# Expert outputs kept by slot and gathered at the end, in place of a scatter that adds into the residual

## Chip, cores and metric

One core of one Trainium2 chip runs the whole program. The metric is the device time of one execution in microseconds (us); a lower number is better. The engines are TensorE (PE, with its weight loads as PEld), VectorE (DVE), ScalarE (ACT), GpSimd (POOL) and SyncE (SP). Every engine executes its own instructions in order. DMAs are issued by SP (queue q1 of the profile) or by POOL (queue q0); both kinds run on the same 16 DMA engines.

## The reference, cut to what matters

One decoder layer over 1,024 tokens and 16 meta tokens, with 1,024 features: a token mixer (attention beside a gated delta rule), a layer norm, a mixture of experts, and a last layer norm. The change concerns the mixture of experts and what follows it. Each token takes one of four groups and in it two of eight experts, so each of the 1,024 tokens has two (expert, weight) pairs out of 32 experts.

```
combine = group_onehot[:, :, None] * (g_val * within)[:, None, :]
y = jnp.zeros((t, x.shape[1]), jnp.float32)
for gi in range(N_GROUPS):
    h = jax.nn.silu(x @ w1[sl]) * (x @ w3[sl])
    y = y + jnp.einsum("tef,efd->td", h * combine[:, gi, :, None], w2[sl])
...
h = layer_norm(DEEPNORM_ALPHA * h + ffn, ln2_g[i], ln2_b[i])
```

## The kernel before

Everything is float32; for TensorE each operand is split into a rounded high part and a low rest, and three products are summed. The last third of the program is `phase4`, and it is written in a fixed order (a manual schedule), not chosen by a scheduler.

Routing gives each (token, choice) pair a slot: `pose` is its place in its expert's list, `oh` its expert as a one-hot row, `ix[:, e]` the token that stands in each of the 128 slots of expert `e` (a number past the end for an empty slot), `gsl` the weight of that slot. On average 64 of 128 slots are filled (2,048 pairs over 32 experts). An expert with more than 128 tokens would go through a separate branch (`overflow`), which is compiled in and not taken with these inputs.

The expert loop runs over `e` from 0 to 31. The token rows of expert `e` are fetched by an indirect DMA from `h1d`, the layer's normalised rows in DRAM (`gather`, L1498, three buffers `xg`). PE transposes them, multiplies by w1 and w3 (`up`), ACT and DVE make the SwiGLU, and `down` multiplies by w2. The weights, 3 MiB for each expert, come in three 1 MiB loads by SP (`load_raw`, L1449) into a ring of 17 tiles, so up to 5.67 experts ahead; ACT and DVE split them into high and low parts. In the pass for `e` the product of expert `e - 1` is weighted and copied into one of two buffers `y` (`evac`, ACT L1566 and DVE L1567), and POOL sends it off (`scatter`, L1571): an indirect DMA that adds 128 rows of `y` into the rows of `res` in DRAM. `res` was filled earlier with the same rows as `h1d`.

The outputs of the last two experts (30 and 31) are not scattered. They stay on chip, and PE adds them in the last stage by a product with one-hot matrices (`pf`, L1738).

The last stage, `finish`, takes eight tiles of 128 tokens. SP loads `yt0` to `yt7` from `res` after the last scatter (L1637). For a tile, `total` adds `pf` and sums the row (DVE L1747), `square` (ACT L1751, L1752), `rstd` (DVE L99, POOL L100), `shift` (DVE L1758), `scale` (ACT), `gain` (DVE L1764), and `store` (an add on DVE or POOL, L1767, and SP's store L1768). The list `TO` sets the stagger of these steps over the tiles, and `TV` names the tiles whose last add is on DVE.

Between the loop and `finish` stands the branch for overflow (`If(nv > 0)`, L1662). Where it isn't taken, POOL still waits for its own DMAs and then raises the semaphores by what the branch would have raised (INC_SWDGE_SEM).

Of the kernel before, what the change touches and what calls it, by code (L numbers as in the profile page):

```python
# [17 lines left out]
P = 128  # L18
D = 1024
# [17 lines left out]
TV, TO = (4, 6, 7), (0, 0.75, 1.25, 2.5, 3.25, 4, 4.75)  # L37
# [9 lines left out]
YB = 2  # L47
SPK = ()
# [31 lines left out]
class Trunk:  # L80
# [738 lines left out]
    def phase2(self):  # L819
# [242 lines left out]
        self.res = self.dram.tile([SEQ, D], F32, name="res")  # L1062
# [107 lines left out]
        def s1(t):  # L1170
            c = T[t]
            ht = c["ht"]
            for s in range(2):
                omm(t, s, 0, 1.0)
                yield
            if t < 6:
                rs = self.ln_stats(ht, P)
                self.ln_apply(ht, P, rs, ht)
                for v, w in ((O["g1"], ALU.mult), (O["b1"], ALU.add)):
                    nc.vector.tensor_tensor(ht, ht, v, op=w)  # L1180
            else:
                c["st"] = mv, rs = self.ln_stats(ht, P, raw=True)
                yield
                nc.vector.scalar_tensor_tensor(rs[:, 1:2], mv[:, 0:1], -1.0, rs[:, 0:1], op0=ALU.mult, op1=ALU.mult)
                self.ln_apply(ht, P, rs, ht)
                for v, w in ((O["g1"], ALU.mult), (O["b1"], ALU.add)):
                    for h in range(2):
                        (nc.gpsimd if h in LH[t - 6] else nc.vector).tensor_tensor(
                            ht[:, h * F:(h + 1) * F], ht[:, h * F:(h + 1) * F], v[:, h * F:(h + 1) * F], op=w)
            nc.sync.dma_start(self.h1d[t * P:(t + 1) * P, :], ht)  # L1190
            nc.sync.dma_start(self.res[t * P:(t + 1) * P, :], ht)
# [282 lines left out]
    def phase4(self):  # L1474
# [155 lines left out]
        g2, b2 = [fp.tile([P, D], F32, name=n) for n in ("g2", "b2")]  # L1630
        for v, n in ((g2, "ln2_g"), (b2, "ln2_b")):
            (nc.gpsimd if GQ else nc.sync).dma_start(v, self.bcast(a[n], D))
        yts = [fp.tile([P, D], F32, name=f"yt{t}") for t in range(NT)]

        def load_res(eng):
            for t in range(NT):
                eng.dma_start(yts[t], self.res[t * P:(t + 1) * P, :])  # L1637

        load_res(nc.sync)
        ys.append([fp.tile([P, D], F32R, name=f"y{x}") for x in "hl"])  # L1640
# [17 lines left out]
    def overflow(self, item, ps, xo, reload):  # L1658
# [3 lines left out]
        with tc.If(nv > 0), self.pool("ovf", "left") as vp:  # L1662
# [20 lines left out]
            nc.vector.scalar_tensor_tensor(sl, q, -128.0, pose, op0=ALU.mult, op1=ALU.add)  # L1683
            pa = ps.tile([P, 512], F32, name="py", bufs=3)
# [28 lines left out]
            nc.gpsimd.memset(xo, 0.0)  # L1713
            xi = vp.tile([P, 1], I32, name="xi")
            xg = vp.tile([P, 1], F32, name="xg")
            with tc.For_i(0, nv) as i:
# [3 lines left out]
                nc.vector.tensor_copy(xg, g16[:, bass.ds(i, 1)])  # L1720
                item(a["w13"][bass.ds(ev, 1)].rearrange("o p k f -> p (o k) f"),
                     a["w2"][bass.ds(ev, 1)].rearrange("o p k f -> p (o k) f"),
                     xi, xg, xo)
            reload(nc.gpsimd)

    def finish(self, fp, g2, b2, yts, oh, ys, sq):
# [3 lines left out]
        with self.psum("psf") as ps, tc.manual_schedule():  # L1730
# [26 lines left out]
            def shift(t):  # L1757
                nc.vector.tensor_tensor(rs[t][:, 1:2], st[t][:, 1:2], rs[t][:, 0:1], op=ALU.mult)  # L1758
# [73 lines left out]
```

## Time and profile before

| what | us |
|---|---|
| median of 3 runs | 1203.93 (1203.56 to 1207.17) |
| the profiled execution, its own time | 1209.06 |
| its span, first to last instruction | 1207.3 |
| PE busy | 1086.3 |
| DVE busy | 865.7 |
| ACT busy | 625.4 |
| POOL busy | 308.6 |

The profiled execution's own time is 1.8 us over its span and 5.1 us over the median. Busy times are sums over the program; what a change in the expert loop or in the last stage is worth is read from those stretches, about 830 to 1160 and 1160 to 1207 of the span.

### The profile page before, as it was taken

To read this page: it belongs to the slowest core of one execution; us is meant where nothing else is said; L and a number is where in the kernel's file an instruction comes from. 1 tells how busy PE (TensorE), PEld (TensorE's weight loads), DVE (VectorE), ACT (ScalarE), POOL (GpSimd) and SP (SyncE) were. 2 spreads that over 40 slices of the span, in tenths; PEclk is the share of its full clock that TensorE was granted. 3 is DMA by queue.
4 is the path that set the end of the run, shared out by engine and by line. 5 is a ranking of instruction groups with operands and counts; after the bars stand their busy time and mean duration, and the time that the engine had idled before them with its cause. 6 is when DMAs were issued, how large, how long until landed. Compare 5 with 4: busy or idle time off the path is not lost. (4 is left out here: it accounts for less than half of the span.)

```text
span 1207.3 us, 19744 instructions
## 1 busy us (share of the span) xinstructions
PE 1086.3 (90%) x7029; PEld 925.2 (77%) x7029; DVE 865.7 (72%) x1661; ACT 625.4 (52%) x1310; POOL 308.6 (26%) x380
## 2 busy tenths in 40 slices
PE   6999999999899979899899999839999889888981
PEld 4999999999899958778677777837776666666761
DVE  7941357989433248999757687778988787787978
ACT  3443346845223245655456463236776566566854
POOL 3523103402000023444333230011222122122315
PEclk9999999999989979999979999769999999999996
DMA  7411124465896577876657653957999999997453
GB/s 284 175 62 45 50 93 125 150 189 188 241 253 187 171 259 213 250 233 190 196 133 187 239 181 114 401 220 256 359 335 328 316 321 320 321 323 265 83 195 139
DMA packets 111287, 259.22 MB, mean 215 GB/s; under 512 B 32804, under 2 KB 62252, under 8 KB 98386
## 3 DMA queue, kind: packets, MB, share of 16 engines
q1 hardware_dynamic: 101680, 239.57, 59.0%
q0 software_dynamic: 9216, 17.28, 6.2%
q8 instruction: 57, 0.93, 0.3%
q10 hardware_dynamic: 290, 1.07, 0.2%
q14 instruction: 44, 0.36, 0.1%
HBM read 205.44 MB, written 68.72 MB: 227 GB/s over the span
## 5 line engine op out<-in xcount | busy, mean ns | idle before, releaser
L184 PE MATMUL pj<-hTh,wfh 128*128 128x346 f32 (+1 forms) x480 | 156.5, 326 | 0.0
L186 PE MATMUL pj<-hTh,wfl 128*128 128x346 f32 (+1 forms) x480 | 156.0, 325 | 0.0
L185 PE MATMUL pj<-hTl,wfh 128*128 128x346 f32 (+1 forms) x480 | 156.0, 325 | 0.0
L1571 POOL DMA_INDIRECT res<-y,ix x30 | 51.0, 1699 | 234.7 <-DVE y L1567 168.0
L879 DVE TENSOR_TENSOR_SCAN mm<-mm,zero 128x272 f32<-128x272 f32 (+3 forms) x64 | 89.6, 1413 | 20.8 <-ACT mm L866 18.4
L184 PEld LDWEIGHTS pj<-hTh,wfh 128*128 128x128 f32 x480 | 91.1, 190 | 0.4 <-issue 0.3
L185 PEld LDWEIGHTS pj<-hTl,wfh 128*128 128x128 f32 x480 | 91.1, 190 | 0.2
L186 PEld LDWEIGHTS pj<-hTh,wfl 128*128 128x128 f32 x480 | 91.1, 190 | 0.1
L1462 DVE TENSOR_TENSOR w13l<-raw,w13h 128x512 fp32r<-128x512 f32 x144 | 88.9, 684 | 0.0
L1530 PE MATMUL ph<-w13h,xh 128*128 128x512 f32 x192 | 88.5, 461 | 0.0
L177 PE MATMUL pj<-wvh,hTl 128*128 128x256 f32 (+3 forms) x280 | 79.1, 285 | 3.6 <-DVE hTl L95 3.6
L176 PE MATMUL pj<-wvl,hTh 128*128 128x256 f32 (+3 forms) x280 | 79.1, 285 | 2.2 <-DVE wvl L95 2.2
L175 PE MATMUL pj<-wvh,hTh 128*128 128x256 f32 (+3 forms) x280 | 79.7, 288 | 0.2 <-ACT hTh L94 0.2
L1461 ACT ACTIVATE w13h<-raw 128x512 fp32r<-128x512 f32 x144 | 77.8, 625 | 0.0
L1532 PE MATMUL ph<-w13h,xl 128*128 128x512 f32 x192 | 75.1, 391 | 0.0
L1531 PE MATMUL ph<-w13l,xh 128*128 128x512 f32 x192 | 74.9, 390 | 0.0
L864 PE MATMUL z<-qk 128*128 128x416 f32 (+6 forms) x224 | 60.7, 378 | 7.0 <-ACT kuw L776 4.4
L866 ACT ACTIVATE mm<-z 128x512 f32<-128x512 f32 (+1 forms) x80 | 44.2, 565 | 42.0 <-PE z L864 36.8
L870 POOL TENSOR_SCALAR_AFFINE_SELECT mm<-mm 128x128 f32<-128x128 f32 x64 | 36.5, 576 | 114.6 <-ACT mm L866 114.2
L94 ACT ACTIVATE xh<-tp 128x512 fp32r<-128x512 f32 x64 | 31.4, 490 | 58.8 <-DVE xf L1517 53.0
L1462 DVE TENSOR_TENSOR w2l<-raw,w2h 128x512 fp32r<-128x512 f32 x96 | 60.0, 687 | 2.3 <-ACT w2h L1461 0.2
L900 ACT ACTIVATE wt<-tp 128x512 f32<-128x512 f32 (+1 forms) x80 | 41.6, 556 | 27.9 <-PE tp L899 27.3
(425 smaller groups left out, 2932.6 us busy)
## 6 DMA issues: line engine op xcount, KB each, us to landing
raw<-in_w SPq DMA_DIRECT2D x72, 1024.0 KB
qk<-qkd SPq DMA_DIRECT2D x16, 520.0 KB
ht<-hscr SPq DMA_DIRECT2D x16, 512.0 KB
qk<-qkd SPq DMA_DIRECT2D x16, 392.0 KB
kqvd<-y SPq DMA_DIRECT2D x12, 520.0 KB
wfr<-in_w_gdn SPq DMA_DIRECT2D x12, 512.0 KB
wo4h<-in_w SPq DMA_DIRECT2D x6, 1024.0 KB
wo4l<-in_w SPq DMA_DIRECT2D x6, 1024.0 KB
```

The source lines that it names most:

```text
L175: nc.tensor.matmul(o[:p, :n], xh, wh[:, kt, ws], start=(kt == 0), stop=False)
L176: nc.tensor.matmul(o[:p, :n], xh, wl[:, kt, ws], start=False, stop=False)
L177: nc.tensor.matmul(o[:p, :n], xl, wh[:, kt, ws], start=False, stop=(kt == KT - 1))
L184: nc.tensor.matmul(o[:, :n], wh[:, kt], self.hTh[:, kt, c0:c0 + n], start=(kt == 0), stop=False)
L185: nc.tensor.matmul(o[:, :n], wh[:, kt], self.hTl[:, kt, c0:c0 + n], start=False, stop=False)
L186: nc.tensor.matmul(o[:, :n], wl[:, kt], self.hTh[:, kt, c0:c0 + n], start=False, stop=(kt == KT - 1))
L879: nc.vector.tensor_tensor_scan(mm[:, c0:c1][:, ::-1], mm[:, c0:c1][:, ::-1], self.zero1.to_broadcast([P, c1 - c0]), 1.0, op0=ALU.mult, op1 ...
L1461: nc.scalar.activation(wh, raw, AF.Copy)
L1462: (nc.gpsimd if k in pool else nc.vector).tensor_tensor(wl, raw, wh.bitcast(F32), op=ALU.subtract)
L1530: nc.tensor.matmul(ph, xh[:, kt], wh, start=False, stop=False)
L1531: nc.tensor.matmul(ph, xh[:, kt], wl, start=False, stop=False)
L1532: nc.tensor.matmul(ph, xl[:, kt], wh, start=False, stop=(kt == ks[-1]))
```

## The change

Expert outputs no longer go into the residual's rows. `ysd` is a new DRAM tensor of 30 x 128 rows; `keep` stores the whole `y` of expert `e` as rows `e * 128` to `e * 128 + 127`, with a plain DMA from POOL. `res` and its eight stores are gone. `fi` holds, for each token and choice, its row in `ysd` (128 x expert + slot, or past the end where the expert is 30 or 31); DVE computes it in five instructions before the loop. In the last stage SP loads `yt` from `h1d`, and `combine` adds two rows for each token of a tile with two indirect DMAs whose destination is `yt` in on-chip memory. Five tiles (`GE`) are combined ahead of the overflow branch, the other three from inside `shift`. All eight last adds go to DVE. The gather for a later expert moves behind the transposes of its pass, and the loads of the gain and bias rows move from POOL to SP.

```
-TV, TO = (4, 6, 7), (0, 0.75, 1.25, 2.5, 3.25, 4, 4.75)
+TV, TO = (0, 1, 2, 3, 4, 5, 6, 7), (0, 0.75, 1.25, 2.5, 3.25, 4, 4.75)
+GE = 5
...
-        self.res = self.dram.tile([SEQ, D], F32, name="res")
+        self.ysd = self.dram.tile([(NE - 2) * P, D], F32, name="ysd")
+        self.ovd = self.dram.tile([16 * P, D], F32, name="ovd")
...
-            nc.sync.dma_start(self.res[t * P:(t + 1) * P, :], ht)
...
-        def scatter(y, yi):
-            nc.gpsimd.indirect_dma_start(out=self.res, out_offset=bass.IndirectOffsetOnAxis(ap=yi, axis=0),
-                                         in_=y, in_offset=None, bounds_check=SEQ - 1, oob_is_err=False,
-                                         compute_op=ALU.add)
+        def keep(y, e):
+            nc.gpsimd.dma_start(self.ysd[e * P:(e + 1) * P, :], y)
+
+        def combine(src, fi, n, t):
+            for k in range(2):
+                nc.gpsimd.indirect_dma_start(out=yts[t], out_offset=None, in_=src,
+                                             in_offset=bass.IndirectOffsetOnAxis(ap=fi[:, t, k:k + 1], axis=0),
+                                             bounds_check=n * P - 1, oob_is_err=False, compute_op=ALU.add)
...
+        nc.vector.tensor_tensor(ev, self.oh, self.slots[:, None, None, :NE].to_broadcast([P, NT, 2, NE]), op=ALU.mult)
+        nc.vector.tensor_reduce(fv, ev, axis=AX, op=ALU.add)
+        nc.vector.scalar_tensor_tensor(fv, fv, float(P), self.pose, op0=ALU.mult, op1=ALU.add)
+        nc.vector.tensor_scalar(fo, self.pose, float(P), 4096.0, op0=ALU.is_ge, op1=ALU.mult)
+        nc.vector.tensor_tensor(fi, fv, fo, op=ALU.add)
         xt = xsplit(xpose(XB[0]))
+        gat_(XN)
...
         for e in range(NE):
-            gat_(e + XN)
...
+                gat_(e + 1 + XN)
...
-                    yo, yi = down(act, pcs.pop(e - 1)), self.ix[:, e - 1:e]
-                    scatter(evac(yo, self.gsl[:, e - 1:e]), yi)
+                    keep(evac(down(act, pcs.pop(e - 1)), self.gsl[:, e - 1:e]), e - 1)
...
+        for t in range(NT):
+            nc.sync.dma_start(yts[t], self.h1d[t * P:(t + 1) * P, :])
...
+        for t in range(GE):
+            combine(self.ysd, fi, NE - 2, t)
         evac2(down(act, pcs.pop(NE - 1)), self.gsl[:, NE - 1:], ys[1])
...
-        self.finish(fp, g2, b2, yts, oh, ys, sq)
+        self.finish(fp, g2, b2, yts, oh, ys, sq, lambda t: t < NT and combine(self.ysd, fi, NE - 2, t))
...
             def shift(t):
+                more(t + GE)
                 nc.vector.tensor_tensor(rs[t][:, 1:2], st[t][:, 1:2], rs[t][:, 0:1], op=ALU.mult)
```

POOL at the end of the expert loop, before: the scatters of experts 27 to 29 (each waits for DVE, ACT and one DMASW, the semaphore of the scatter ahead of it) and the two row loads.

```order
L1571 DMA res<-y,ix 1024x1024 [waits DMASW1_49,DVE_49,Activation_49]
L1571 DMA res<-y,ix 1024x1024 [waits DMASW3_49,DVE_49,Activation_49]
L1571 DMA res<-y,ix 1024x1024 [waits DMASW4_49,DVE_49,Activation_49]
L1632 DMA g_12653<-in_ln_g 128x1024 [waits DMAHW2_49,DMAHW1_49,DMAHW6_49,DMAHW0_49,DMAHW7_49,DMASW6_49,DVE_49]
L1632 DMA b_12654<-in_ln_b 128x1024
```

The same place after the change: the stores of experts 27 to 29, then the gathers for tiles 0 to 4, of which tiles 0, 1 and 4 are shown (`yt_12597`, `yt_12598`, `yt_12601`). DMASW names with other numbers than the neighbour's are older DMAs that used the same semaphore.

```order
L1572 DMA ysd<-y 128x1024 [waits DVE_49,Activation_49]
L1572 DMA ysd<-y 128x1024 [waits DMASW4_49,DVE_49,Activation_49]
L1572 DMA ysd<-y 128x1024 [waits DMASW5_49,DVE_49,Activation_49]
L1576 DMA yt_12597<-ysd,fi 128x1024 [waits DMAHW2_49,DMASW6_49,DMAHW3_49,DMASW5_49,DMAHW4_49,DMASW4_49,DMAHW5_49,DMASW3_49,DMAHW6_49,DMASW2_49,DMASW0_49]
L1576 DMA yt_12597<-ysd,fi 128x1024 [waits DMASW7_49,DMASW6_49]
L1576 DMA yt_12598<-ysd,fi 128x1024 [waits DMAHW5_49]
L1576 DMA yt_12598<-ysd,fi 128x1024 [waits DMASW1_49,DMASW0_49]
...
L1576 DMA yt_12601<-ysd,fi 128x1024 [waits DMAHW2_49,DMAHW3_49,DMAHW1_49,DMAHW0_49]
L1576 DMA yt_12601<-ysd,fi 128x1024 [waits DMASW7_49,DMASW6_49]
```

Now the first gather of a tile waits for the stores or only for its `yt` load, and the second waits for the first of the same tile (the DMASW semaphore that the row ahead of it raises).

POOL in the last stage, before: the wait at the end of the untaken branch, then a power (L100) for each tile, and from the fourth on the adds of tiles 0 to 3 between them.

```order
L1662 ISA [waits Pool_49,DMASW4_49,DMASW5_49,DMASW3_49,DMASW6_49,DMASW2_49,DMASW7_49,DMASW1_49,DMASW0_49]
L1662 UNCONDITIONAL_BRANCH
L100 TENSOR_TENSOR rs_13008<-rs_13008,mhalf 128x1 [waits DMAHW5_49,DMAHW6_49,DMAHW4_49,DMAHW7_49,DMAHW3_49,DVE_49]
L100 TENSOR_TENSOR rs_13009<-rs_13009,mhalf 128x1 [waits DVE_49]
L100 TENSOR_TENSOR rs_13010<-rs_13010,mhalf 128x1 [waits DVE_49]
L100 TENSOR_TENSOR rs_13011<-rs_13011,mhalf 128x1 [waits DVE_49]
L1767 TENSOR_TENSOR yt_12657<-yt_12657,b_12654 128x1024 [waits DMAHW4_49,DMAHW5_49,DMAHW3_49,DMAHW6_49,DMASW7_49,PE_49]
```

After the change, the same place: the wait at the branch, two powers, and the gathers of tiles 5 to 7 (`yt_12602` to `yt_12604`) with one power ahead of each further pair.

```order
L1676 ISA [waits Pool_49,DMASW4_49,DMASW5_49,DMASW3_49,DMASW6_49,DMASW2_49,DMASW7_49,DMASW1_49,DMASW0_49]
L1676 UNCONDITIONAL_BRANCH
L101 TENSOR_TENSOR rs_13044<-rs_13044,mhalf 128x1 [waits DVE_49]
L101 TENSOR_TENSOR rs_13045<-rs_13045,mhalf 128x1 [waits DVE_49]
L1576 DMA yt_12602<-ysd,fi 128x1024 [waits DMAHW1_49,DMASW7_49,DMASW2_49]
L1576 DMA yt_12602<-ysd,fi 128x1024 [waits DMASW3_49,DMASW2_49]
L101 TENSOR_TENSOR rs_13046<-rs_13046,mhalf 128x1 [waits DVE_49]
L1576 DMA yt_12603<-ysd,fi 128x1024 [waits DMAHW2_49,DMASW4_49,DMAHW3_49,DMASW0_49,Activation_49]
L1576 DMA yt_12603<-ysd,fi 128x1024 [waits DMASW5_49,DMASW4_49]
L101 TENSOR_TENSOR rs_13047<-rs_13047,mhalf 128x1 [waits DVE_49]
L1576 DMA yt_12604<-ysd,fi 128x1024 [waits DMAHW3_49,DMASW6_49,DMASW1_49]
L1576 DMA yt_12604<-ysd,fi 128x1024 [waits DMASW6_49]
```

Six gathers moved in between POOL's powers, and the wait at the branch now has ten gathers ahead of it instead of scatters and row loads. The third place is DVE's last stage. Before, the first `total` waits for the load of its tile (DMAHW4), for a semaphore that POOL raises at the branch (DMASW2) and for PE; behind the last `total` (tile 7) stand a gain, the small steps and another gain.

```order
L1747 SCALAR_TENSOR_TENSOR yt_12657,st_13000<-pf,yt_12657 128x1024 [waits DMAHW4_49,DMASW2_49,PE_49]
L1747 SCALAR_TENSOR_TENSOR yt_12658,st_13001<-pf,yt_12658 128x1024 [waits DMAHW5_49,DMASW3_49,PE_49]
...
L1747 SCALAR_TENSOR_TENSOR yt_12664,st_13007<-pf,yt_12664 128x1024 [waits DMAHW3_49,DMASW1_49,PE_49]
L1764 TENSOR_TENSOR yt_12660<-yt_12660,g_12653 128x1024 [waits Activation_49]
L99 TENSOR_SCALAR rs_13014<-st_13006 128x1 [waits Activation_49]
L1758 TENSOR_TENSOR rs_13013<-st_13005,rs_13013 128x1 [waits Pool_49]
L1764 TENSOR_TENSOR yt_12661<-yt_12661,g_12653 128x1024 [waits Activation_49]
```

After the change, the same rows (the file's lines are some 27 further down), where the first waits for tile 0's second gather (DMASW7) and, as before, for what POOL raises at the branch.

```order
L1773 SCALAR_TENSOR_TENSOR yt_12597,st_13036<-pf,yt_12597 128x1024 [waits DMASW7_49,DMASW2_49,PE_49]
L1773 SCALAR_TENSOR_TENSOR yt_12598,st_13037<-pf,yt_12598 128x1024 [waits DMASW3_49,DMASW1_49,PE_49]
...
L1773 SCALAR_TENSOR_TENSOR yt_12604,st_13043<-pf,yt_12604 128x1024 [waits DMASW7_49,PE_49]
L1791 TENSOR_TENSOR yt_12600<-yt_12600,g_12593 128x1024 [waits Activation_49]
L100 TENSOR_SCALAR rs_13050<-st_13042 128x1 [waits Activation_49]
L1785 TENSOR_TENSOR rs_13049<-st_13041,rs_13049 128x1 [waits Pool_49]
L1794 TENSOR_TENSOR yt_12600<-yt_12600,b_12594 128x1024 [waits DVE_49]
```

Behind the last `total` (tile 7) DVE has the gains and the adds of tiles 3 to 7, ten instructions of 128x1024; before, five gains and three adds stood there.

## Rows read from the trace of the kernel before

**Rows 1.** Span of the core and its mean granted clock.

```profile
core 0: 1207.3 us, clock 0.954
```

**Rows 2.** Waits between 830 and 1130 us: total, times, longest (us).

```profile
ACT y L1566 <- DMA res<-y,ix: 43.3, 20, 2.9
DVE y L1567 <- DMA res<-y,ix: 27.7, 16, 2.4
```

**Rows 3.** Timeline of POOL: start us, us, what, [idle before <-releaser].

```profile
885.39 1.58 POOL L1571 DMA_INDIRECT res<-y,ix  x1 [8.21 <-ACT y L1566]
...
897.41 1.59 POOL L1571 DMA_INDIRECT res<-y,ix  x1 [9.09 <-DVE y L1567]
899.31 1.04 POOL L1498 DMA_INDIRECT xg<-h1d,ix  x1 [0.31 <-PE ph L1532]
...
1113.61 1.59 POOL L1571 DMA_INDIRECT res<-y,ix  x1 [8.43 <-DVE y L1567]
```

**Rows 4.** The scatter's line alone: from issue to landing.

```profile
DMA to landing us min/median/max: 5.8/10.5/12.3
```

**Rows 5.** Timeline of ACT: the copies of `y` for experts 2, 3, 6 and 29.

```profile
854.93 0.68 ACT L1566 ACTIVATE y<-py,gsl 128x512 f32<-128x512 f32 x1
864.59 0.68 ACT L1566 ACTIVATE y<-py,gsl 128x512 f32<-128x512 f32 x1
896.62 0.69 ACT L1566 ACTIVATE y<-py,gsl 128x512 f32<-128x512 f32 x1 [2.85 <-DMA res<-y,ix]
1149.83 0.69 ACT L1566 ACTIVATE y<-py,gsl 128x512 f32<-128x512 f32 x1
```

**Rows 6.** Stretches: us, busy time by engine, granted clock, DMA share, GB/s.

```profile
760.00:770.00 10.00, 10.00 (x50) 9.96 (x49) 4.96 (x19) 1.79 (x3) 0.00 (x0) 0.50 1.01 424
860.00:870.00 10.00, 10.00 (x48) 7.65 (x47) 9.59 (x19) 7.89 (x17) 4.66 (x2) 1.00 0.98 356
1140.00:1150.00 10.00, 10.00 (x47) 7.69 (x46) 9.59 (x18) 7.88 (x17) 1.95 (x1) 1.00 0.24 39
```

**Rows 7.** DMA queues from 830 to 895: packets, MB, share of 16 engines.

```profile
q1 hardware_dynamic: 2738, 19.99, 81.3%
q0 software_dynamic: 1354, 2.11, 14.3%
```

**Rows 8.** Timeline of POOL at the end of the loop, loads done.

```profile
1136.05 1.74 POOL L1571 DMA_INDIRECT res<-y,ix  x1 [4.30 <-DVE w13l L1462]
1143.09 1.95 POOL L1571 DMA_INDIRECT res<-y,ix  x1 [5.31 <-DVE w2l L1462]
1152.28 1.88 POOL L1571 DMA_INDIRECT res<-y,ix  x1 [7.24 <-ACT w2h L1461]
1154.84 0.62 POOL L1632 DMA_DIRECT2D g<-in_ln_g  x1 [0.68 <-DVE w2l L1462]
```

**Rows 9.** Timeline at the first gather and at the transpose that reads it.

```profile
810.07 1.34 POOL L1498 DMA_INDIRECT xg<-h1d,ix  x1 [16.77 <-DVE ob L1428]
...
814.59 1.94 PE L1508 MATMUL tp<-ident,xg 128*128 128x128 f32 x8 [5.85 <-DMA xg<-h1d,ix]
```

**Rows 10.** DMA issues: the second row load by POOL, KB, us to landing.

```profile
b<-in_ln_b POOLq DMA_DIRECT2D x1, 512.0 KB, 7.1
```

**Rows 11.** The branch's line: POOL's raise of the semaphores, ns, start us.

```profile
L1662 POOLq INC_SWDGE_SEM x1: 356/356/356, 1162.7 to 1162.7; - x1
```

**Rows 12.** Timelines of DVE and POOL: last evacuation of `y`, and the last stage.

```profile
1150.72 0.75 DVE L1567 TENSOR_SCALAR y<-py,gsl 128x512 f32<-128x512 f32 x1 [0.28 <-PE py L1560]
...
1169.29 1.23 DVE L1747 SCALAR_TENSOR_TENSOR yt<-pf,yt 128x1024 f32<-128x1024 f32 x1 [3.71 <-PE pf L1738]
...
1202.42 1.23 DVE L1767 TENSOR_TENSOR yt<-yt,b 128x1024 f32<-128x1024 f32 x1
...
1173.68 0.55 POOL L100 TENSOR_TENSOR rs<-rs,mhalf 128x1 f32<-128x1 f32 x1 [0.78 <-DVE rs L1758]
```

**Rows 13.** DMA queue q0 from 1143 to 1150, one scatter and nothing else.

```profile
q0 software_dynamic: 144, 0.30, 28.1%
```

More of the change, by code (lines that the diff above doesn't have):

```diff
@@ L1589, in phase4 @@
             gat_(e)
+        fi = self.small.tile([P, NT, 2], I32, name="fi", bufs=1)
+        eo = mp.tile([P, D], F32, name="y", bufs=YB)
+        ev = eo[:, :2 * NT * NE].rearrange("p (t k e) -> p t k e", t=NT, k=2)
+        fv, fo = [eo[:, D - 2 * NT * (i + 1):D - 2 * NT * i].rearrange("p (t k) -> p t k", k=2) for i in range(2)]
+        nc.vector.tensor_tensor(ev, self.oh, self.slots[:, None, None, :NE].to_broadcast([P, NT, 2, NE]), op=ALU.mult)
[3 more added lines that the diff above has]
+        nc.vector.tensor_tensor(fi, fv, fo, op=ALU.add)
         xt = xsplit(xpose(XB[0]))
+        gat_(XN)
         self.load_raw(2 + RC - RX)
@@ L1630, in phase4, with item @@
         g2, b2 = [fp.tile([P, D], F32, name=n) for n in ("g2", "b2")]
+        ys.append([fp.tile([P, D], F32R, name=f"y{x}") for x in "hl"])
+        yts = [fp.tile([P, D], F32, name=f"yt{t}") for t in range(NT)]
+        for t in range(NT):
+            nc.sync.dma_start(yts[t], self.h1d[t * P:(t + 1) * P, :])
         for v, n in ((g2, "ln2_g"), (b2, "ln2_b")):
[L1632 to L1640, printed above, removed]
+            nc.sync.dma_start(v, self.bcast(a[n], D))
+        for t in range(GE):
+            combine(self.ysd, fi, NE - 2, t)
         evac2(down(act, pcs.pop(NE - 1)), self.gsl[:, NE - 1:], ys[1])
         self.man.close()
-        def item(w13, w2, xi, gv, x):
+        def item(w13, w2, xi, gv, x, yi):
             gather(x, xi)
@@ L1647, in item @@
             self.split_k(loads(w13, w2), range(12), p)
-            scatter(evac(down(apose(swiglu(up(xsplit(xpose(x)), p))), p), gv), xi)
-        self.overflow(item, ps, yts[0], load_res)
+            y = evac(down(apose(swiglu(up(xsplit(xpose(x)), p))), p), gv)
+            nc.gpsimd.indirect_dma_start(out=self.ovd, out_offset=bass.IndirectOffsetOnAxis(ap=yi, axis=0),
+                                         in_=y, in_offset=None, bounds_check=16 * P - 1, oob_is_err=False)
+        self.overflow(item, ps, fp.tile([P, D], F32, name="xo"), combine)
         pss.close()
         sq = mp.tile([P, KT, P], F32R, name="xh", bufs=1).rearrange("p a b -> p (a b)")
-        self.finish(fp, g2, b2, yts, oh, ys, sq)
+        self.finish(fp, g2, b2, yts, oh, ys, sq, lambda t: t < NT and combine(self.ysd, fi, NE - 2, t))
         fin.close()
@@ L1656, in phase4, with overflow @@
         self.wos.close()
-    def overflow(self, item, ps, xo, reload):
+    def overflow(self, item, ps, xo, combine):
         nc, tc, a = self.nc, self.tc, self.a
@@ L1683, in overflow @@
             nc.vector.scalar_tensor_tensor(sl, q, -128.0, pose, op0=ALU.mult, op1=ALU.add)
+            fo = vp.tile([P, NT, 2], F32, name="fo")
+            nc.vector.tensor_scalar(fo, q, 0.0, 65536.0, op0=ALU.is_equal, op1=ALU.mult)
+            nc.vector.tensor_tensor(fo, fo, sl, op=ALU.add)
+            fi = vp.tile([P, NT, 2], I32, name="fi")
+            nc.vector.scalar_tensor_tensor(fi, it, float(P), fo, op0=ALU.mult, op1=ALU.add)
+            yv = vp.tile([P, 16], I32, name="yv")
+            nc.gpsimd.iota(yv, pattern=[[P, 16]], base=0, channel_multiplier=1)
             pa = ps.tile([P, 512], F32, name="py", bufs=3)
@@ L1713, in overflow @@
             nc.gpsimd.memset(xo, 0.0)
+            for i in range(16):
+                nc.gpsimd.dma_start(self.ovd[i * P:(i + 1) * P, :], xo)
             xi = vp.tile([P, 1], I32, name="xi")
             xg = vp.tile([P, 1], F32, name="xg")
+            yi = vp.tile([P, 1], I32, name="yi")
             with tc.For_i(0, nv) as i:
@@ L1720, in overflow, with finish @@
                 nc.vector.tensor_copy(xg, g16[:, bass.ds(i, 1)])
+                nc.vector.tensor_copy(yi, yv[:, bass.ds(i, 1)])
                 item(a["w13"][bass.ds(ev, 1)].rearrange("o p k f -> p (o k) f"),
                      a["w2"][bass.ds(ev, 1)].rearrange("o p k f -> p (o k) f"),
-                     xi, xg, xo)
-            reload(nc.gpsimd)
-    def finish(self, fp, g2, b2, yts, oh, ys, sq):
+                     xi, xg, xo, yi)
+            for t in range(NT):
+                combine(self.ovd, fi, 16, t)
+    def finish(self, fp, g2, b2, yts, oh, ys, sq, more):
         nc, tc = self.nc, self.tc
```

## Prediction

> **What bounds the kernel now.** I first looked where the end is decided: the span is 1207.3 us [rows 1], and its last 375 us are the expert loop (about 830 to 1160) and the last stage. In the waits of the loop the only long stalls of ACT and DVE that a DMA ends are those of `y` on the scatter, 43.3 and 27.7 us in total [rows 2]. POOL's timeline tells why. From the scatter at 885.39 to that at 1113.61 lie twenty, so one starts every 11.41 us [rows 3]; a scatter takes 10.5 us (median) from issue to landing [rows 4], and by its semaphore each waits for the one ahead. 10.5 us and some 0.9 to restart POOL are the whole period. The row at 897.41 names DVE as the releaser, but DVE's `y` was itself released by the same landing (ACT's copy of `y` at 896.62 waited 2.85 us for it [rows 5]). So the loop is bound by a chain of scatters, one at a time.
>
> Without that chain the pace is seen at the start, where two `y` buffers still hide it: 854.93 to 864.59 is 9.66 us for an expert [rows 5], with PE busy 10.00 of 10 us at the full clock (1.00, the 2.4 GHz level). From 1140 to 1150, with the DMA share down at 0.24, PE is again at 10.00 of 10 [rows 6]. PE bounds the loop then.
>
> **What the change takes away.** A store into rows of its own needs no predecessor; POOL's rows after the change show it waiting for DVE, ACT and older DMAs alone. At 9.66 us the copy of `y` of expert 29 would come 26 periods after 864.59, at 1115.8, where it now comes at 1149.83 [rows 5]: **34.1 us gained**. A `y` buffer is written again two experts (19 us) after its store, and even the slowest scatter landed in 12.3 [rows 4].
>
> Three things are costed at nothing. The five DVE instructions for `fi` lie between 810.07 and 814.59, where DVE has nothing to do until PE transposes the first gather [rows 9]; uncovered they cost 2 us, estimated from the 1.23 us of an instruction over 1024 columns [rows 12]. The eight removed stores to `res` lie ahead of the loop, which waits for routing there. The loads of `yt` now need no scatter, and go out while the loop still runs.
>
> DMA is the doubt. In the stretch at full pace (830 to 895) q1 moved 19.99 MB in 81.3% of 65 us, 2.64 us for a MB on all engines, and q0 2.11 MB in 14.3%, 4.41 us for a MB [rows 7]. An expert will need 3.15 MB of weights (8.3 us), 0.26 of gather and 0.52 of store, since empty slots are stored too. At q1's price for both that is 10.4 us, at q0's price, which holds the adding scatters, 11.8. Both exceed 9.66, but the ring holds 5.67 experts, 55 us. Over the 26 remaining experts the deficit is 19 us at the low price, which the ring covers, and 56 at the high one, which it just fails to. Plain traffic alone ran at 424 GB/s [rows 6], 9.3 us for 3.93 MB, so I take the low price and no loss.
>
> **What the change adds.** Sixteen gathers on POOL, each pair in sequence: the second of a tile can't be issued until the first has landed, and POOL issues in order, so the next tile's first stands behind it. Call L the time from the start of a gather to that of an instruction which waits for it, and i the time to the next that doesn't.
>
> - i: 897.41 to 899.31, 1.9 us [rows 3].
> - L: no gather here adds into on-chip memory. Nearest is the scatter with the loads done: 1136.05 to 1143.09, 7.04 us [rows 8], including POOL's restart. From below: the first plain gather started PE 4.52 us after its own start [rows 9]; POOL's restart adds 0.8 (DVE's last `y` ended at 1151.47 [rows 12], the scatter started at 1152.28 [rows 8]): 5.3. From above: that scatter moved 0.30 MB in 28.1% of 7 us, 1.97 us of all engines [rows 13]; a gather fills all 128 rows, 0.52 MB, so 1.5 us more: 8.5. I take 7.0, since it is an adding DMA of the same row size.
> - Start S: expert 29's `y` ends at 1151.47 - 34.1 = 1117.4. The store starts 0.3 later (as the row load at 1154.84 behind its DVE release [rows 8]), lands in about 5 us (bounds 3.65, the last output store, from 1203.65 to the span's end [rows 1, 12], and 7.1 for a row load by POOL [rows 10]), and POOL restarts in 0.8: S = 1123.5.
> - Five tiles ahead: 4(L + i) + 2L = 6L + 7.6 = 49.6. POOL then passes the branch, where it waits for all its DMAs before it raises the semaphores (before, at 1162.7 [rows 11]). DVE's first `total` waits for that too, so nothing of the last stage starts sooner: 1173.1.
> - Tiles 5 to 7: the first of these gathers stands behind the second power, 4.4 us after the first `total` (1169.29 to 1173.68 [rows 12]) and 0.8 for restart: 5.2. Then three pairs: 4L + 2(1.9 + 0.7), a power of 0.55 [rows 12] between them: 33.2. Last landing: 1211.5.
> - Behind it: one `total` and ten gains and adds at about 1.2 us (1.23 [rows 12]), 13.2, and 3.65 for the last store.
>
> **The sum.** 1211.5 + 13.2 + 3.65 = 1228.4 against a span of 1207.3: 21 us lost. In general it is 34.1 us gained and 10L - 15 lost; L = 4.9 is the point of no change. The profiled execution stands 5 us above the median of the runs, so the sum goes on the median: 1203.9 + 21 = **1225**.
>
> Here a rule of the Trainium skill speaks the other way. The trace gives 7.04 us for a quiet adding scatter and 4.52 for a plain gather up to its reader [rows 8, 9]. "DMA: Bandwidth & Descriptors", section "Anatomy of one DMA — SWDGE (gpsimd) path", fits a DMA from GpSimd as 2.0 us and its bytes at 436 GB/s, which for 0.52 MB is an estimate of 3.2 us, with POOL's restart L = 4.0. By it the sum would be 9 us faster than before, 1195; both rows are above it.
>
> **Rivals.**
> - *Faster: the gathers land quickly.* Place: the sixteen waits of POOL. If an adding gather lets POOL go on as soon as the plain one let PE (L = 4.5 [rows 9]), the sum is 25 us less: 1200. For it: the destination is on chip, not DRAM. Against: POOL's restart comes on top, and twice the rows are moved. It decides below L = 4.9. The fit cited above belongs here.
> - *No change:* L between 4.8 and 5.3, at 1203 to 1208.
> - *Slower still: DMA takes over the loop.* At 11.8 us for an expert the loads end some 1.5 us an expert later than I allow once the ring is empty; a third to a half of the 34.1 us is lost: 1225 + 15 = 1240. For it: the share is already 0.98 at 356 GB/s [rows 6]. Against: the adding scatters, q0's dear part, are gone.
> - *The loop doesn't get faster at all,* the chain being replaced by another wait on `y`: 1225 + 34 = 1259. Nothing in the new waits shows one.
>
> **How the numbers follow.** Runs differ by 0.3%, about 3.6 us, which is also what can be told from no change. My forecast (L from 5.3 to 8.5: 1208 to 1240, likeliest 1225) has 0.74; quick gathers 0.09; no change 0.05; DMA-bound 0.10; no gain in the loop 0.02. Faster 0.09, same 0.06 (a little of the forecast's lower edge), slower 0.85. The range 1206 to 1242 leaves out the quick gathers and the far ends of the slow cases.
>
> **What would show it.** In the changed profile: copies of `y` every 9.66 us up to expert 29 at about 1116, with no wait for a DMA; the first gather into `yt` at about 1123, pairs 7 and 1.9 us apart; the first `total` near 1173, not before the tenth gather has landed; six more gathers between POOL's powers, the last landing near 1211, and DVE alone behind it. The prediction is wrong if L is under 5, if the first `total` starts while the first five tiles are still being gathered, or if PE waits for weights in the loop.

## The result, and the profile after

| | before | after |
|---|---|---|
| median of the runs taken side by side, us | 1205.55 (4 runs) | 1243.13 (4 runs) |
| ratio to before, 95% interval | | 1.0295 (1.0245 to 1.0346) |
| span of the profiled execution, us | 1207.3 | 1241.9 |

The change makes the kernel slower by 37.6 us, where 21 were forecast. In the rows, the expert loop gained what was said and the last stage lost more than was said.

**The loop.** Busy time of the engines from 895 to 1080 (PE, weight loads, DVE, ACT, POOL, then granted clock, DMA share and GB/s), after the change:

```profile
895.00:1080.00 185.00, 185.00 (x844) 141.56 (x844) 176.83 (x326) 144.14 (x288) 31.18 (x38) 1.00 1.00 401
```

The DMA queues there (packets, MB, share of 16 engines):

```profile
q1 hardware_dynamic: 8078, 58.79, 78.5%
q0 software_dynamic: 5558, 15.27, 21.6%
```

The same stretch before:

```profile
895.00:1080.00 185.00, 165.94 (x721) 119.18 (x720) 150.58 (x275) 118.97 (x245) 44.26 (x33) 1.00 0.94 323
```

PE has no pause in 185 us, at the full clock, where it stood still for 19 us before; the DMA engines are full at 401 GB/s (before, a share of 0.94 with 323 GB/s). ACT's copies of `y` for the first and the last stored expert, after, and for the first one before:

```profile
837.19 0.68 ACT L1567 ACTIVATE y<-py,gsl 128x512 f32<-128x512 f32 x1
...
1117.45 0.69 ACT L1567 ACTIVATE y<-py,gsl 128x512 f32<-128x512 f32 x1
```

```profile
835.48 0.68 ACT L1566 ACTIVATE y<-py,gsl 128x512 f32<-128x512 f32 x1
```

After, 29 periods take 280.26 us, 9.66 each; before, from 835.48 to 1149.83 [rows 5], 314.35. The loop gained 34.1 us, and since it began 1.7 us later, its last copy comes 32.4 us sooner.

**The last stage.** POOL's timeline (start, duration, operation, in brackets its idle time and what ended it) from the last store to the fifth gather, and from the twelfth gather on:

```profile
1119.62 0.53 POOL L1572 DMA_DIRECT2D ysd<-y  x1 [9.13 <-ACT ah L95]
1123.65 4.92 POOL L1576 DMA_INDIRECT yt<-ysd,fi  x1 [3.49 <-issue]
1138.01 1.58 POOL L1576 DMA_INDIRECT yt<-ysd,fi  x1 [9.44 <-DMA yt<-ysd,fi]
1139.89 1.56 POOL L1576 DMA_INDIRECT yt<-ysd,fi  x1 [0.30 <-issue]
1147.61 1.56 POOL L1576 DMA_INDIRECT yt<-ysd,fi  x1 [6.16 <-DMA yt<-ysd,fi]
1149.47 1.57 POOL L1576 DMA_INDIRECT yt<-ysd,fi  x1 [0.30 <-issue]
...
1193.88 1.56 POOL L1576 DMA_INDIRECT yt<-ysd,fi  x1 [4.98 <-DMA yt<-ysd,fi]
1194.93 1.13 POOL L101 TENSOR_TENSOR rs<-rs,mhalf 128x1 f32<-128x1 f32 x1
1196.24 2.65 POOL L1576 DMA_INDIRECT yt<-ysd,fi  x1 [0.18 <-issue]
1205.96 1.59 POOL L1576 DMA_INDIRECT yt<-ysd,fi  x1 [7.07 <-DMA yt<-ysd,fi]
1207.02 1.15 POOL L101 TENSOR_TENSOR rs<-rs,mhalf 128x1 f32<-128x1 f32 x1
1208.34 2.62 POOL L1576 DMA_INDIRECT yt<-ysd,fi  x1 [0.17 <-issue]
1218.56 1.58 POOL L1576 DMA_INDIRECT yt<-ysd,fi  x1 [7.60 <-DMA yt<-ysd,fi]
```

Each second gather waits for the first of its tile. The first one needs 14.36 us to the next (1123.65 to 1138.01), the three after that 7.72, 7.72 and 7.33 (1159.07 to 1166.40), those of tiles 6 and 7 9.72 and 10.22. DVE's first and last `total`, and POOL's wait in the untaken branch:

```profile
1182.04 1.22 DVE L1773 SCALAR_TENSOR_TENSOR yt<-pf,yt 128x1024 f32<-128x1024 f32 x1 [48.63 <-DMA yt<-ysd,fi]
...
1224.72 1.23 DVE L1773 SCALAR_TENSOR_TENSOR yt<-pf,yt 128x1024 f32<-128x1024 f32 x1 [2.65 <-DMA yt<-ysd,fi]
```

```profile
L1676 POOLq INC_SWDGE_SEM  x1: 356/356/356, 1181.7 to 1181.7; - x1
```

DVE did nothing for 48.63 us; its first `total` comes 0.3 us after the branch's wait ended (1181.7), though tile 0's second gather was issued at 1138.01 and such gathers land some 6.4 us after issue. From 1140 to 1180 the DMA engines, too, were only partly busy:

```profile
1140.00:1180.00 40.00, 1.70 (x8) 1.04 (x6) 0.00 (x0) 0.00 (x0) 12.40 (x8) 0.58 0.63 107
```

Since the loop begins sooner or later from one execution to the next (its first gather at 804.25 in one of the changed kernels below, at 814.11 in another), I measure the last stage from ACT's copy of `y` of expert 29 to the end of the span. Before it is 57.5 us (1149.83 [rows 5] to 1207.3), after 124.5 (1117.45 to 1241.9). Predicted was 112.6 (1115.8 to 1228.4).

### The profile page after: what moved, and what is told of

Same layout as the page of the kernel before. It is cut to its first block, busy times and chain, and to the rows that moved or that the text cites. A ratio compares the mean times of both kernels' runs of the same rounds, so it can differ in the third digit from the quotient of the medians.

```text
span 1241.9 us, 19751 instructions
## 1 busy us (share of the span) xinstructions
PE 1079.4 (87%) x7029; PEld 930.2 (75%) x7029; DVE 863.0 (69%) x1671; ACT 631.0 (51%) x1310; POOL 292.4 (24%) x389
## 5 line engine op out<-in xcount | busy, mean ns | idle before, releaser
L1499 POOL DMA_INDIRECT xg<-h1d,ix x32 | 34.0, 1063 | 170.5 <-PE tp L1509 133.3
L871 POOL TENSOR_SCALAR_AFFINE_SELECT mm<-mm 128x128 f32<-128x128 f32 x64 | 39.3, 619 | 115.4 <-ACT mm L867 115.2
L178 PEld LDWEIGHTS pj<-wvh,hTl 128*128 128x128 f32 (+1 forms) x280 | 52.7, 188 | 3.5 <-DVE hTl L96 3.1
```

What stands on the lines that cost most here:

```text
L178: nc.tensor.matmul(o[:p, :n], xl, wh[:, kt, ws], start=False, stop=(kt == KT - 1))
```

## The experiments

The first theory: the loop's gain is real; the loss comes from POOL's serial pairs and, separately, from the wait at the branch. Rivals: the DMA engines' rate of adding rows sets the time (A); only the slow first gather does (B); the loop's gain is not passed on (C).

**1. No gathers at all.**

```
-        for t in range(GE):
-            combine(self.ysd, fi, NE - 2, t)
...
-        self.finish(fp, g2, b2, yts, oh, ys, sq, lambda t: t < NT and combine(self.ysd, fi, NE - 2, t))
+        self.finish(fp, g2, b2, yts, oh, ys, sq, lambda t: None)
```

> All sixteen gathers are left out (the outputs of experts 0 to 29 are then missing from the sum); the stores and everything else stay. It shows what the loop alone gains. Theory (the loop gains its 32 to 34 us, and the gathers cost all of the loss): POOL passes the branch by 1127, the first total starts by 1136, the span ends at 1170 to 1180. Rival C (the loop's gain is not passed on to the end, because loads or PE are late there): the span ends at 1195 or later.

Span 1168.3; the copy of expert 29 at 1114.31, so 54.0 us to the end (a single run, 1.7 us under the expected range). Rival C falls: the sixteen gathers cost 70.5 of the 124.5 us.

**2. First rows of five tiles, then second rows.**

```
-        for t in range(GE):
-            combine(self.ysd, fi, NE - 2, t)
+        for k in range(2):
+            for t in range(GE):
+                combine(self.ysd, fi, NE - 2, t, (k,))
```

> The ten gathers ahead of the branch are reordered: first rows of tiles 0 to 4, then second rows of tiles 0 to 4, so that only the sixth has a wait for a gather. Theory (the waits of each pair on POOL, and the branch wait behind them, cost the time; a gather takes 6 to 8 us to land but several can be in flight): the ten are issued some 1.9 us apart, the first total moves from 1182.0 to about 1158 (ten times the 2.6 us that I allow for an adding gather's own transfer, from about 1132), the time falls by some 24 us to about 1219, ratio to the kernel before about 1.01. Rival A (the DMA engines' rate of adding rows is the bound, so a gather costs the 4.6 us that it costs on average now, however it is issued): the first total stays between 1178 and 1184 and the time within 5 us of 1243, ratio 1.03. Rival B (only the slow first gather matters): as rival A, since the first gather is not touched.

Ratio 1.0082 (1.0050 to 1.0113), median 1217.97 us; 101.3 us from the copy to the end, 23.2 less. POOL's gathers ahead of the branch:

```profile
1120.17 4.92 POOL L1576 DMA_INDIRECT yt<-ysd,fi  x1 [3.49 <-issue]
1125.38 1.58 POOL L1576 DMA_INDIRECT yt<-ysd,fi  x1 [0.30 <-DMA yt<-h1d]
1127.27 1.56 POOL L1576 DMA_INDIRECT yt<-ysd,fi  x1 [0.30 <-issue]
1129.13 1.56 POOL L1576 DMA_INDIRECT yt<-ysd,fi  x1 [0.30 <-issue]
1130.99 1.57 POOL L1576 DMA_INDIRECT yt<-ysd,fi  x1 [0.30 <-issue]
1133.81 1.57 POOL L1576 DMA_INDIRECT yt<-ysd,fi  x1 [1.24 <-DMA yt<-ysd,fi]
1136.26 1.56 POOL L1576 DMA_INDIRECT yt<-ysd,fi  x1 [0.88 <-DMA yt<-ysd,fi]
1138.45 1.56 POOL L1576 DMA_INDIRECT yt<-ysd,fi  x1 [0.64 <-DMA yt<-ysd,fi]
```

Up to five are in flight, and the first `total` is at 1155.59. Rivals A and B fall for the changed kernel. But the second rows come 2.2 to 2.5 us apart and not 1.9, each ended by a landing: a rate begins to show.

**3. Pairs in sequence, but behind the branch; and both together.** `combine` leaves the place ahead of the branch and `shift`, and becomes two more steps of the staggered list in `finish`. Only their two offsets, at the end of the list `TO`, differ between these kernels (order kept; second rows behind the first rows of the next two tiles; second rows one place sooner, for experiment 7):

```
-            ops = (total, square, rstd, shift, scale, gain, store)
+            ops = (total, square, rstd, shift, scale, gain, store, lambda t: more(t, 0), lambda t: more(t, 1))
-TO = (0, 0.75, 1.25, 2.5, 3.25, 4, 4.75)
+TO = (0, 0.75, 1.25, 2.5, 3.25, 4, 4.75, -1.6, -1.55)
+TO = (0, 0.75, 1.25, 2.5, 3.25, 4, 4.75, -3.6, -1.0)
+TO = (0, 0.75, 1.25, 2.5, 3.25, 4, 4.75, -4.6, -2.0)
```

> All gathers behind the branch, but each tile's second gather right behind its first, so that POOL waits for every pair as in the changed kernel. With the kernel that reorders the gathers ahead of the branch (1218) and the one that does both (1196) it makes four combinations of order and place. Theory (the pairs' waits and the wait at the branch are two separate losses): the first total starts at about 1140 in place of 1182, but pairs still take 9.3 us each, so the last of eight lands near 1203 and the span ends near 1214, ratio about 1.005. Rival I (the branch wait is the whole loss, the pairs' waits are hidden once the last stage runs beside them): as the kernel that does both, 1193 to 1198. Rival J (the place doesn't matter since the gathers set the end either way): within 5 us of 1241.

> All sixteen gathers move behind the untaken branch, the first row of a tile two to three gathers ahead of its second row, POOL's powers between them, so that total of a tile waits for its own two gathers alone. Theory: POOL passes the branch at about 1124, the first total starts at about 1140, a tile follows every 5 to 6 us, the last gather lands near 1178 and the span ends near 1190; ratio to the kernel before 0.98 to 0.99. Rival A (4.6 us for each gather however issued): the last gather lands near 1124 + 16 x 4.6 = 1198, the end is near 1213, ratio 1.00 to 1.01. Rival B (the first gather's 14 us is the main loss and the rest is fixed): gain of at most 9 us over the changed kernel, ratio 1.02.

| gathers | pairs in sequence | second rows apart from the first |
|---|---|---|
| ahead of the branch | 124.5 us, ratio 1.0295 | 101.3 us, 1.0082 (1.0050 to 1.0113) |
| behind the branch | 111.4 us, 1.0209 (1.0160 to 1.0258) | 82.6 us, 0.9895 (0.9867 to 0.9922) |

(Times from the copy of expert 29 to the end, of the profiled executions.) Both losses exist: the order is worth 23.2 us alone and 28.8 with the place changed, the place 13.1 and 18.7; by the medians 25 and 38, and 10 and 22. Rivals I and J fall. Pairs behind the branch came out 17 us slower than I had written. The first `total` is at 1146.21, 6 us later than expected; the seven pairs from 1139.98 to 1207.49 took 9.64 us each where 9.3 were expected; so the last `total` comes at 1214.04, 11 us late. Behind it I had allowed 11 us, and it took 17.3: the 13 of gains and adds and 4 of the store, which stand in the prediction itself. With both changes the first `total` came at 1138.83, the last at 1175.96 and the end at 1193.2, close to what was expected; this version beats the kernel before by 1%.

**4. What a gather's time is made of.** Three kernels: no add; the four last loads behind a DVE copy that reads `yts[0]`; the two comparisons that make `oh` behind the last `evac2`.

```
-   bounds_check=n * P - 1, oob_is_err=False, compute_op=ALU.add)
+   bounds_check=n * P - 1, oob_is_err=False)
```

```
-        for t in range(NT):
+        for t in range(NT - 2):
             nc.sync.dma_start(yts[t], self.h1d[t * P:(t + 1) * P, :])
-        for v, n in ((g2, "ln2_g"), (b2, "ln2_b")):
-            nc.sync.dma_start(v, self.bcast(a[n], D))
...
         evac2(down(act, pcs.pop(NE - 1)), self.gsl[:, NE - 1:], ys[1])
+        nc.vector.tensor_copy(yts[NT - 2][:, :1], yts[0][:, :1])
+        (the four loads: tiles 6 and 7, gain, bias)
```

```
-                for i in (1, 0):
-                    nc.vector.tensor_tensor(oh[i], ..., op=ALU.is_equal)
...
         evac2(down(act, pcs.pop(NE - 1)), self.gsl[:, NE - 1:], ys[1])
+        (the two comparisons)
```

> The gathers overwrite their tile instead of adding to it (this leaves the residual and one of the two expert outputs out of the sum); order and waits stay. It measures what the adding itself costs of the 7.4 to 7.7 us from a gather's start to the next that waits for it. Theory (mostly fixed delay of one DMA from POOL): 6.0 to 6.8 us, the span falls by 5 to 11 us, to 1231 to 1237. Rival A (the adding is the cost): about 4.5 us as the plain gather at the start of the loop, the span falls by 25 us or more, to about 1215.

> SP's last four loads (tiles 6 and 7, gain and bias rows, 2 MB together) go out only when tile 0 is combined, so that they can't stand in the first gather's way; all else as in the changed kernel. The question is why its first gather takes 14.4 us to the next one where the others take 7.4 to 7.7: POOL's own instruction is 3.3 us longer and what follows it 3.3 us longer. Theory D (the loads on the same DMA engines make the second part): from the end of the first gather's instruction to the start of the second falls from 9.4 to about 6.2 us, the instruction stays at 4.9, the whole falls to about 11 us. Theory E (first use of this kind of DMA, or descriptors that are late): both parts stay, 14.4 us.

> DVE's two comparisons over 1024 columns that make the one-hot matrices move behind the last copies of the loop, so that DVE has 2.4 us less to do while POOL writes the first gather's descriptors. Theory F (POOL's instruction is stretched while DVE works without a pause): the instruction falls from 4.92 to 2.5 to 3 us, and the time from its end to the next start stays at 9.4. Theory E (first use): 4.9 stays.

The group of L1576, landing time from issue, after the change and without the add:

```profile
DMA to landing us min/median/max: 5.9/6.4/14.0
```

```profile
DMA to landing us min/median/max: 4.2/4.4/12.4
```

The second tile's two gathers without the add:

```profile
1135.16 1.00 POOL L1576 DMA_INDIRECT yt<-ysd,fi  x1 [0.30 <-issue]
1140.62 1.00 POOL L1576 DMA_INDIRECT yt<-ysd,fi  x1 [4.46 <-DMA yt<-ysd,fi]
```

Without the add a first gather takes 5.5 us to its second (1135.16 to 1140.62) in place of 7.3 to 7.7, and 99.5 us lie between the copy of expert 29 (1114.81) and the end (1214.3), 25.0 less. The adding costs about 2 us a gather, more than my theory allowed (0.6 to 1.7 between these starts), and the start lies between the two expectations (6.0 and 4.5), the span at rival A's. Over a quarter of such a wait is the add.

The same two kernels tell what the add costs on the DMA engines. In stretches with nothing but gathers on them, the row of queue q0 reads, after the change from 1142 to 1175, and without the add from 1136 to 1160:

```profile
q0 software_dynamic: 1086, 3.70, 64.3%
```

```profile
q0 software_dynamic: 1114, 3.81, 50.4%
```

That is 3.70 MB in 64.3% of 33 us, 174 GB/s at a full share, against 3.81 MB in 50.4% of 24 us, 315 GB/s: the same gathers take 1.8 times as long with the add.

The first two gathers with the late loads, and with the late comparisons:

```profile
1124.34 4.91 POOL L1576 DMA_INDIRECT yt<-ysd,fi  x1 [3.49 <-issue]
1134.46 1.58 POOL L1576 DMA_INDIRECT yt<-ysd,fi  x1 [5.22 <-DMA yt<-ysd,fi]
```

```profile
1118.33 2.64 POOL L1576 DMA_INDIRECT yt<-ysd,fi  x1 [3.49 <-issue]
1132.03 1.58 POOL L1576 DMA_INDIRECT yt<-ysd,fi  x1 [11.06 <-DMA yt<-ysd,fi]
```

Theory D holds: without 2 MB of loads beside it the wait behind the instruction is 5.22 us in place of 9.44, and 10.1 us in all. It saves 1.6 us in the end (122.9 from the copy at 1118.13 to 1241.0), since the loads then meet later gathers (1146.62 to 1156.42, 9.80 us). Theory F is right on the instruction, 2.64 in place of 4.92 us, but not on the rest: the wait behind it grew from 9.44 to 11.06, since the gather lands only when the loads are through. Beside the loads the stretched instruction was mostly hidden. Without them it counts. This is the stretch of the kernel with the late loads in which that instruction ran (1124.34 to 1129.25):

```profile
1123.30:1129.30 6.00, 4.87 (x22) 3.57 (x20) 5.16 (x8) 1.43 (x4) 4.91 (x1) 1.00 0.00 0
```

The DMA engines (the last two figures) moved nothing until the instruction had ended, and the 10.1 us are still 2.7 above the 7.4 of an undisturbed gather. Rival E (first use) falls as the cause of either part; no kernel here took away the loads and the stretch together, so that nothing else remains is not shown.

**5. The gathers of tiles 6 and 7.** In `finish`:

```
-                nc.sync.dma_start(self.out[0, t * P:(t + 1) * P, :], yts[t])
...
                 ops[i](t)
+            for t in (7, 0, 1, 2, 3, 4, 5, 6):
+                nc.sync.dma_start(self.out[0, t * P:(t + 1) * P, :], yts[t])
```

> The changed kernel with its eight output stores held back until tile 7 is done (the end itself then comes later, by what seven more stores take; only the gathers are to be read). In the changed kernel the first gathers of tiles 6 and 7 take 9.7 and 10.2 us to the next instead of 7.4 to 7.7: 1.1 us of it is POOL's own instruction, 2.6 in place of 1.6 us beside an add of DVE; 0.9 to 1.4 us more lie behind it. Theory M (the output stores share the DMA engines with these gathers): from the end of their instruction to the next start falls from 7.07 and 7.60 to about 6.2 us, the instruction stays at 2.6. Rival N (the second gather of the tile before is still being transferred): 7.0 to 7.6 stay.

```profile
1197.88 2.66 POOL L1576 DMA_INDIRECT yt<-ysd,fi  x1 [0.18 <-issue]
1205.44 1.59 POOL L1576 DMA_INDIRECT yt<-ysd,fi  x1 [4.90 <-DMA yt<-ysd,fi]
...
1207.81 2.63 POOL L1576 DMA_INDIRECT yt<-ysd,fi  x1 [0.17 <-issue]
1215.30 1.58 POOL L1576 DMA_INDIRECT yt<-ysd,fi  x1 [4.86 <-DMA yt<-ysd,fi]
```

Theory M holds and rival N falls: the waits behind the instruction are 4.90 and 4.86 us in place of 7.07 and 7.60, shorter than the 6.2 expected. The two take 7.56 and 7.49 us in all, as the undisturbed ones do, though POOL's instruction still takes 2.6; so the stores made the whole excess.

**6. What bound the loop before.** The kernel before with two residual tensors, taken in turn (the second starts at zero, POOL adds it behind the branch, and the gain and bias rows come by SP), and with a scatter that overwrites.

```
-                    scatter(evac(yo, self.gsl[:, e - 1:e]), yi)
+                    scatter(evac(yo, self.gsl[:, e - 1:e]), yi, (self.res, self.res2)[e % 2])
...
-                                         in_=y, in_offset=None, bounds_check=SEQ - 1, oob_is_err=False,
-                                         compute_op=ALU.add)
+                                         in_=y, in_offset=None, bounds_check=SEQ - 1, oob_is_err=False)
```

> The kernel before with one change to its chain: experts of even number add into one residual tensor, those of odd number into a second one that starts at zero, so a scatter waits for the one two experts ago; the last stage adds the second tensor's rows (eight plain adding loads by POOL behind the branch). Theory (the loop before was bound by the chain of adding scatters, one at a time): copies of y every 9.7 us, the one of expert 29 at 1114 to 1120 instead of 1149.8, the first total near 1140, the span ends at 1178 to 1190, ratio 0.975 to 0.985. Rival G (the DMA cost of adding scatters, 11.8 us an expert by queue q0's price, would bound the loop as well): copies over 10.5 us apart once the ring is empty, expert 29 after 1130, the span ends past 1195. Rival H (something else than the chain set the 11.4 us): the copies stay 11.4 us apart and the time at 1205 or above.

> The kernel before, whose scatters overwrite rows of the residual instead of adding to them (this leaves the sum of experts out); the chain, each scatter waiting for the one ahead, stays. It asks what the adding is worth in the loop. Theory (adding makes both the chain's period and the DMA work, as the two separate chains showed): landing falls from 10.5 us to 7 to 8.5, below the 9.66 us of PE's pace, the copies of y come every 9.7 to 10 us, the scatter of expert 29 starts at 1115 to 1125 instead of 1152.3, the span ends near 1170 to 1180. Rival L (the chain's period is a fixed delay of indirect DMAs): landing stays above 10, the scatter of expert 29 after 1145, the span above 1200.

Two chains: ratio 0.9973 (0.9938 to 1.0008). Busy times of two stretches, and ACT's copy of expert 29:

```profile
895.00:1040.00 145.00, 145.00 (x663) 110.91 (x662) 138.80 (x256) 112.92 (x225) 49.80 (x30) 1.00 0.94 322
1040.00:1130.00 90.00, 83.11 (x358) 61.28 (x356) 72.96 (x134) 59.89 (x120) 23.11 (x20) 0.96 0.91 316
```

```profile
1141.79 0.69 ACT L1572 ACTIVATE y<-py,gsl 128x512 f32<-128x512 f32 x1 [0.20 <-PE py L1566]
```

Up to 1040 PE runs without a pause, so the chain was the wait before. Behind 1040 PE is at 83.11 of 90 us: the ring of weights has run empty, as the DMA engines moved only 322 GB/s up to there. From the waits between 1040 and 1130:

```profile
ACT w13h L1467 <- DMA raw<-in_w: 12.6, 11, 1.8
```

So rival G's limit stands right behind the chain, from the point where the ring is empty, and its figures came: a span past 1195 (1210.2), and the copy of expert 29 after 1130, if barely so without the late start of this execution told below. From the first copy (847.08) to the last 294.7 us pass, 19.6 less than before, of 34.1. The last stage gives 10.9 back (68.4 in place of 57.5), and this execution's loop began 11.6 us later than before's, which no run here explains (the changed kernels differ among themselves by up to 10 us in it). With the overwriting scatter the chain stays, and the queues from 895 to 1080 read:

```profile
q1 hardware_dynamic: 8044, 58.58, 83.5%
q0 software_dynamic: 5357, 9.40, 13.6%
...
res<-y,ix POOLq DMA_INDIRECT x19, 9.1
```

The copy of expert 29 comes at 1118.49, the span is 1176.0. Landing, the last figure of the third row, is 9.1 us in place of 10.5 [rows 4], above the 7 to 8.5 expected but below PE's 9.66 us, and no copy of `y` waited for a scatter; and q0 needs 13.6% of the engines for 9.40 MB, where two chains needed 20.2% for 9.34. So the adding made both limits: the chain's period and the DMA work.

**7. A better version.** The last line of offsets above; and, with it, a gain and add right behind the next tile's `total`.

> As the kernel with all gathers behind the branch, but each tile's second gather one place sooner, ahead of the power of three tiles before, so that POOL doesn't wait for DVE's power while a gather could be issued. Theory (POOL's order still costs time there, 3.75 us for each gather against 2.6 us of transfer that I allow): the last gather lands at about 1168 to 1172 instead of about 1178, the span ends at 1183 to 1189, ratio 0.98 to 0.985. Rival A (the rate of adding rows on the DMA engines is the bound by now): within 3 us of that kernel's 1193, ratio 0.99.

```
-TO = (0, 0.75, 1.25, 2.5, 3.25, 4, 4.75, -4.6, -2.0)
+TO = (0, 0.25, 0.5, 0.75, 0.8, 1.1, 1.2, -5.35, -2.75)
```

> The kernel with the seconds one place sooner, and a shorter stagger: a tile's gain and last add come right behind the next tile's total, not four tiles later, so that DVE does them while it waits for gathers. Theory: of the 13 us that DVE works behind the last total some 6 to 7 remain; the output stores now share the DMA engines with the gathers, 1.4 us for each of eight, which takes part of it back; the span ends at 1180 to 1185, ratio 0.975 to 0.985. Rival K (the stores' traffic takes all of it back, since the DMA engines are full while the gathers run): within 2 us of 1187 to 1190, ratio 0.988.

The first: ratio 0.9878 (0.9836 to 0.9920), 76.1 us from the copy to the end. By the trace that is 6.5 us better than 82.6, as expected; by the medians (1193.53 and 1195.88 us) the two can't be told apart. The second: 0.9889 (0.9849 to 0.9930), no gain, as rival K said. The queue rows from 1130 to 1160 of the first show why more order doesn't help:

```profile
DMA packets 1761, 5.99 MB, mean 200 GB/s; under 512 B 300, under 2 KB 300, under 8 KB 1760
...
q0 software_dynamic: 1760, 5.98, 104.9%
```

Here rival A is right: the gathers alone fill the DMA engines, at 200 GB/s, half of what plain traffic reached in the loop. How much of that is the add and not the gather, experiment 4 tells (1.8 times). 0.52 MB take 2.6 us, and sixteen 42. (A share over 100% means that packets on one engine overlapped in time.)

## Why the prediction was right, and where a size was off

- **The loop.** Right: 9.66 us for an expert, no wait of `y` for a DMA, and the 34.1 us. The last copy is 1.65 us later than 1115.8, as the loop began 1.65 us later (first gather at 811.72 against 810.07 [rows 9]). The low price for DMA also held: 3.93 MB in 9.66 us are 407 GB/s, and 401 was measured; q0 took 21.6% of 185 us for 15.27 MB, 2.62 us for a MB, where the adding scatters had made it 4.41. The five instructions for `fi` cost nothing, as said: from the first gather to the first copy of `y` 25.4 us pass before and 25.5 after. The prediction told the chain as the whole bound; it was the first of two limits, and the change took both away, as its stores neither wait nor add.
- **Start of the gathers.** 1123.5 predicted, 1123.65 measured, and that close by luck: the last store started 1.9 us later than said (1119.62 against 1117.7), and the gather came 4.0 us behind it in place of 5.8. The store landed in 2.9 us, not 5; the row of its issue:

```profile
ysd<-y POOLq DMA_DIRECT2D x1, 512.0 KB, 2.9
```

- **L, the step that was mis-sized.** The mechanism is the one forecast, the sum 6L + 4i and 4L. I took 7.0 for all of them. The eight times from a first gather to its second are 14.36, 7.72, 7.72, 7.33, 7.38, 6.59, 9.72 and 10.22: 71.0 us in place of 56, while the two landings that a `total` waits for were 6.39 (1175.65 to 1182.04) and 6.16. That is 15.0 - 1.5 = 13.5 us, all of the excess of the span over the sum (1241.9 - 1228.4). The five that had little beside them are 7.35 on average, near 7.0; what I left out was company, above all on the DMA engines. The first gather shared them with SP's 2 MB of loads, which is 4.2 us of its 14.36 (experiment 4); some 2.8 more remain without the loads, with POOL's instruction at 4.9 us beside DVE's work, and no run separates these further. The gathers of tiles 6 and 7 shared the engines with the output stores (experiment 5). Loads and stores were in sight: the change puts the loads there, and a store follows each last add. This carried the time from the middle of the range to its upper end (1203.9 + 37.6 = 1241.5, the median itself 1243.1, against 1242), as the range bounded L by transfers of the gather alone.
- **The branch.** Right: the first `total` waits for all ten (1182.04, 0.3 us behind the wait's end). It is 8.9 us later than 1173.1, 7.4 of them by the first gather.
- **Behind the last landing.** 13.2 predicted, 13.2 measured (1224.72 to the end of the last add); then 4.0 against 3.65.
- **Rivals.** Quick gathers: the fit of the Trainium skill ("DMA: Bandwidth & Descriptors", section "Anatomy of one DMA — SWDGE (gpsimd) path") gives an estimate of 3.2 us for 0.52 MB. The plain store above, alone on the engines, landed in 2.9 us, near it; the overwriting gathers landed in 4.4 us and the adding ones in 6.4 (medians), so for gathers the measurement goes against it here. DMA as the loop's bound did not occur in the changed kernel, but does where the adds stay (experiment 6).

## What to carry to other kernels

Before replacing an adding scatter by gathers at the end, count the end: a chain beside PE costs only what exceeds PE's pace (here 11.41 against 9.66 us for an expert), whereas sixteen gathers behind the loop stand on the path in full. If they must be there, issue the first halves of several tiles ahead of their second halves, so that several gathers are in flight, and put them behind a branch that waits for its engine's DMAs, not ahead of it. Size a DMA wait by what else the DMA engines carry at that moment, and look for a second limit behind the wait that ends last.

## What the runs showed of the hardware

- Adding nearly halves what the DMA engines move: row gathers issued in pairs moved 174 GB/s at a full share with the add and 315 without (experiment 4). Adding gathers with several in flight reached 200 GB/s, the plain traffic of the loop 401. An adding gather of 128 rows of 4 KB lands 2.0 us later than one that overwrites (6.4 and 4.4 us).
- While POOL's instruction for the first gather ran (4.91 us, late loads), the DMA engines moved nothing; the data followed its end.
- POOL's instruction for such a gather takes 1.57 us, or 1.00 without the add, while DVE is idle; 2.6 us beside one DVE add of 1.2 us and 4.9 us beside DVE's unbroken work at the end of the loop. That DVE's work does it is shown for the first gather (4.92 us fell to 2.64 with the comparisons moved, experiment 4); no run here shows by which path the two disturb each other.
